# Seven block products in place of eight for half of the down projections' columns

## The chip, the cores and the metric

One core of a Trainium2 chip runs the whole program. The metric is the device time of one execution in microseconds (us); smaller is better. Weights come from HBM in every execution, as float32.

## What is computed

The reference is a two-layer decoder trunk over one sequence of 256 tokens with a model width of 2048. Each layer adds a mixer (layer 0: sliding-window attention beside a Mamba-2 scan; layer 1: dilated attention) and then an MLP. The change is in the MLPs alone:

```python
def squared_relu_mlp(h, w_up, w_down):
    u = jnp.einsum('bsd,df->bsf', h, w_up)
    return jnp.einsum('bsf,fd->bsd', jnp.square(jax.nn.relu(u)), w_down)

# every layer: x += mixer(rmsnorm(x)); x += squared_relu_mlp(rmsnorm(x))
# h: 256 x 2048, w_up: 2048 x 8192, w_down: 8192 x 2048
```

## The kernel before

**Products in three terms.** Every float32 operand is split in two parts of a shorter format (float32r): a high part, which is a rounded copy, and a low part, the rest. A product is the sum of high·high, high·low and low·high, so each product of a 128x128 block with a 128x512 block is three matmuls of 512 columns.

**Pieces.** `run` (line 229) works through one list, `todo`, of pieces. A piece is two k tiles of a weight (2 x 128 rows) by 512 columns, 512 KB. For each piece the SP queue loads it into `wraw` (`fetch`, line 233; 4 buffers, `RAW`), ScalarE (ACT in the profile) makes the high part `whi` (`high`, line 245; 5 buffers), and VectorE (DVE) subtracts it to make the low part `wlo` (`low`, line 252; 4 buffers). TensorE (PE) then does 12 matmuls: two k tiles, two halves of 128 tokens, three terms. At its place in the list, piece i first issues `low(i+2)`, `fetch(i+6)` and `high(i+3)`, then what is pending from the unit that ended (its `after`), and then its own matmuls.

**Units.** A unit is one 512-column stripe of one projection, all its k tiles in turn, with two PSUM banks `acc` (one for each 128 tokens).

**Side work.** Everything else (norms, attention, the MLP's activation) is a generator in `tasks`. `tick` (line 173), called once for each k tile, advances the tasks that are due, as long as a model of DVE's and ACT's load stays under a limit. `need` (line 187) does not wait for a due time: it advances the tasks in the order of the list, whatever their due times, until a label is in `done`. A unit calls it before the piece that reads what the label stands for. The order in which instructions are issued is the order on every engine's queue, since the scheduling is manual.

**The MLP** (`mlp`, line 847). There are 16 up units (`up(i)`, 8 pieces each) and 8 groups of four down units (`down(i)`, four stripes of 4 pieces, over the 8 k tiles that the up units 2i and 2i+1 give). The order is up 0, up 1, then for i from 1 to 7: up 2i, up 2i+1, down i-1; and down 7 at the end. So a period is 16 up pieces and 16 down pieces. When an up unit ends, `squared` (line 849) runs at its side: ACT applies ReLU from PSUM into `relu`, DVE squares it, PE transposes it in eight 128x128 steps into `uT` (PSUM), and `split` makes the high and low parts `uh` and `ul`. When a down unit ends, `add_stripe` (line 516) adds its two banks to `res`, the residual.

**Buffers.** `slot` tiles (`hThi`, `hTlo`, `uh`, `ul` and the like) share 18 buffers of 4 KB a partition, and `w4` tiles (`relu` and the like) share 11. PSUM has four `acc` banks and four `aux` banks.

Of the kernel before, what the change touches and what calls it, by code (L numbers as in the profile page):

```python
# [7 lines left out]
F32 = mybir.dt.float32  # L8
# [22 lines left out]
RAW = 4  # L31
AHEAD = 3
FREE = 1100.0
LIMIT = 1200.0
CAP = (2, 2, 2, 3)
XZ = ((0, 0), (1, 0), (0, 1), (2, 0), (1, 1), (3, 0), (2, 1), (3, 1))
# [3 lines left out]
def trunk(ctx: ExitStack, tc: tile.TileContext, x, norm_mix, norm_ffn, w_up, w_down, ab_w_in, ab_q_norm,  # L40
# [2 lines left out]
    nc = tc.nc  # L43
    consts = ctx.enter_context(tc.tile_pool(name="consts", bufs=1))
    wpool = ctx.enter_context(tc.tile_pool(name="weights", bufs=4))
    slots = ctx.enter_context(tc.tile_pool(name="slots", bufs=18))
    work = ctx.enter_context(tc.tile_pool(name="work", bufs=11))
    small = ctx.enter_context(tc.tile_pool(name="small", bufs=4))
    accs = ctx.enter_context(tc.tile_pool(name="accs", bufs=4, space=bass.MemoryType.PSUM))
    auxs = ctx.enter_context(tc.tile_pool(name="auxs", bufs=4, space=bass.MemoryType.PSUM))  # L50
# [24 lines left out]
    V, S, PE = Engine(nc.vector, "V", 90, 1.04), Engine(nc.scalar, "S", 240, 0.83), Engine(nc.tensor, "PE", 0, 0.84)  # L75

    def slot(name):
        return slots.tile([128, 4, T], F32R, name=name, tag="slot")

    def w4(shape, name):  # L80
        return work.tile(shape, F32, name=name, tag="w4")
# [88 lines left out]

    load = {"V": 0.0, "S": 0.0}

    def tick():
        clock[0] += 1
        for e in load:
            load[e] = max(0.0, load[e] - FREE)
        ran = []
        while max(load.values()) < LIMIT and len(ran) < 4:
            before = dict(spent)
            t = step(skip=ran)  # L180
            if t is None:
                break
            ran.append(t)
            for e in load:
                load[e] += spent[e] - before[e] - 0.5 * (spent["PE"] - before["PE"])

    def need(label):
        while label not in done:
            assert step(True) or label in done, label
# [30 lines left out]
            V.scalar_tensor_tensor(lo, src, gain, f32(hi), op0=OP.mult, op1=OP.subtract)  # L220


    units = []

    def unit(segs, ktiles, after, flip=False, needs={}):

        units.append((segs, ktiles, after, flip, needs))

    def run():
        todo = [(u, c) for u in units for c in range(0, len(u[1]), KC)]  # L230
        raws, parts = {}, {}

        def fetch(i):
            if i >= len(todo):
                return
            (segs, ktiles, *_), c = todo[i]
            kt = ktiles[c][0]
            raws[i] = raw = wpool.tile([128, KC, sum(s[2] for s in segs)], F32, name="wraw", bufs=RAW)
            o = 0
            for w, c0, m in segs:  # L240
                nc.sync.dma_start(raw[:, :, o:o + m],
                                  w[kt * 128:(kt + KC) * 128, c0:c0 + m].rearrange("(k p) c -> p k c", p=128))
                o += m

        def high(i):
            if i < len(todo):
                raw = raws[i]
                hi = wpool.tile([128, KC, raw.shape[2]], F32R, name="whi", bufs=AHEAD + 2)
                S.activation(hi, raw, AF.Copy)
                parts[i] = [hi]  # L250

        def low(i):
            if i < len(todo):
                raw = raws.pop(i)
                lo = wpool.tile([128, KC, raw.shape[2]], F32R, name="wlo", bufs=AHEAD + 1)
                V.tensor_tensor(lo, raw, f32(parts[i][0]), op=OP.subtract)
                parts[i].append(lo)

        for i in range(RAW):
            if i % 2 == 0:  # L260
                load_x(i // 2)
            fetch(i)
        for i in range(AHEAD):
            high(i)
            low(i)
            if i == 0:
                need(todo[0][0][4][0])
            if i % 2 == 0:
                load_x(2 + i // 2)
            fetch(RAW + i)  # L270
        high(AHEAD)
        nc.sync.dma_start(cst[:, C_TRI:], shapes[:, C_TRI:])
        pending = None
        before = ps = None
        kept, held = [], []
        for i, (u, c) in enumerate(todo):
            segs, ktiles, after, flip, needs = u
            n = sum(s[2] for s in segs)
            if i:
                low(i + AHEAD - 1)  # L280
                fetch(i + AHEAD - 1 + RAW)
                high(i + AHEAD)
            if pending is not None:
                pending[0](pending[1])
                pending = None
            if c == 0:
                if before is not None:
                    need(before)
                before = ps and id(ps)
                ps = [accs.tile([128, W], F32, name="acc") for _ in range(2)]  # L290
                kept.append(ps)
            if c in needs:
                need(needs[c])
            hi, lo = parts.pop(i)
            end = i == len(todo) - 1
            for k in range(KC):
                tick()
                first, last = c + k == 0, c + k == len(ktiles) - 1
                xh, xl, j = ktiles[c + k][1]()
                xh, xl = xh[:, j], xl[:, j]  # L300
                if flip:
                    for b in range(n // 128):
                        o = ps[b // 2][:, (b % 2) * T:(b % 2 + 1) * T]
                        wh, wl = hi[:, k, b * 128:(b + 1) * 128], lo[:, k, b * 128:(b + 1) * 128]
                        PE.matmul(o, wh, xh, start=first and b % 2 == 0, stop=False, skip_group_check=True)
                        PE.matmul(o, wh, xl, start=False, stop=False, skip_group_check=True)
# [12 lines left out]
            if c + KC >= len(ktiles):  # L319
                pending = after, ps  # L320
        pending[0](pending[1])


    class Norm:
# [196 lines left out]
                last(t, j)  # L521
        free(ps)

    def residual_units(w, ktiles, needs={}, nm=None, last=None):
        for j in range(NS):
            def after(ps, j=j):
                add_stripe(ps, j, last)
                if nm is not None:
                    nm.begin(j)

            unit([(w, j * W, W)], ktiles, after, needs=needs if j == 0 else {})


    win, wout = ab_w_in[0], ab_w_out[0]
# [306 lines left out]


    NB = FF // W

    def mlp(layer, nm, nxt, last=None):
        wu, wd = w_up[layer], w_down[layer]
        u = {}

        def squared(i, ps):
            yield from until(("rs", nm.row))  # L850
            r = w4([128, 2, W], "relu")
            for t in range(2):
                S.activation(r[:, t], ps[t], AF.Relu, scale=nm.rs_at(t))
            free(ps)
            yield 2
            V.tensor_tensor(r, r, r, op=OP.mult)
            yield 3
            u[i] = slot("uh"), slot("ul")
            for a in range(2):
                p = aux("uT")  # L860
                for b in range(2):
                    for t in range(2):
                        PE.transpose(p[:, b * T + t * 128:b * T + (t + 1) * 128],
                                     r[:, t, (2 * a + b) * 128:(2 * a + b + 1) * 128], ident)
                yield 1
                p = p.rearrange("p (b t) -> p b t", b=2)
                split(u[i][0][:, 2 * a:2 * a + 2], u[i][1][:, 2 * a:2 * a + 2], p)
                yield 2

        def after_up(i, ps):  # L870
            side(squared(i, ps), ("u", layer, i))

        def up(i):
            unit([(wu, i * W, W)], nm.ktiles(), lambda ps: after_up(i, ps), needs=nm.needs() if i == 0 else {})

        def down(i):
            kts = [(4 * (2 * i + b) + k, (lambda b=b, k=k: u[2 * i + b] + (k,))) for b in range(2) for k in range(4)]
            fin = i == NB // 2 - 1
            residual_units(wd, kts, {4 * b: ("u", layer, 2 * i + b) for b in range(2)}, nxt if fin else None,
                           last if fin else None)  # L880

        up(0)
        up(1)
        for i in range(1, NB // 2):
            up(2 * i)
            up(2 * i + 1)
            down(i - 1)
        down(NB // 2 - 1)

    n2 = Norm(R_MIX + 16, False)  # L890
    mlp(0, n1, n2)
# [111 lines left out]
```

## Time and profile before

| | |
|---|---|
| median of 3 runs | 2324.46 us (2324.34 to 2324.63) |
| profiled execution | 2324.46 us, of which its span (first to last instruction) is 2322.7 us |
| PE busy | 2310.5 us, 99% of the span |
| DVE busy | 1425.4 us, 61% |
| ACT busy | 1100.2 us, 47% |
| HBM read | 420.64 MB, 182 GB/s over the span |

Busy time of an engine is the time in which it had an instruction under way. PE's matmuls are pipelined: one is listed with some 0.39 us, while the next starts 0.23 us after it, so the mean duration of a matmul is not its cost; the distance between two starts is. PEld is the loading of PE's stationary operand, which runs beside the matmuls. PEclk (or PEclk in a view of stretches) is the clock that PE was granted, as a share of 2.4 GHz. A wait "A <- B" is the idle time of engine A that ended when B finished something.

### The profile page before, as it was taken

Reading aid. Unit: us, or ns where it says so; the run is one execution under the profiler, and the core shown is the slowest. Engines: PE = TensorE matmul, PEld = TensorE weight load, DVE = VectorE, ACT = ScalarE, POOL = GpSimd, SP = SyncE. Lnnn points to the kernel's source line nnn. Section 1 sums busy time; section 2 is a strip of 40 time slices with the busy share of each in tenths; the row PEclk is TensorE's granted clock in tenths of the full one; section 3 lists DMA queues with packets and bytes.
Section 4 is the critical chain, followed back from the end, with each engine's and each line's share of the span. In section 5 each row is a group of like instructions: output and inputs, shape, how many; then the busy total and the mean of one; then the engine's idle time right before and its main releaser. Section 6 shows DMA issues by size and latency. Waiting matters only on the chain.

```text
span 2322.7 us, 30056 instructions
## 1 busy us (share of the span) xinstructions
PE 2310.5 (99%) x11317; PEld 1928.3 (83%) x11317; DVE 1425.4 (61%) x2150; ACT 1100.2 (47%) x1411; POOL 8.4 (0%) x20
## 2 busy tenths in 40 slices
PE   8999999999999999999999999999999999999999
PEld 7999988888888888888888778778888888888887
DVE  6779986555555555555566766655555555555554
ACT  5565555444444444444454555554444444444442
POOL 1000000000000000000000000000000000000000
PEclk9999999999999999999999999999999999999999
DMA  7546655566666666666656555546656666656664
GB/s 231 163 145 191 180 174 181 190 188 184 191 187 190 192 183 191 192 188 191 190 179 184 155 154 171 165 160 183 189 185 189 191 189 191 190 184 194 191 185 162
DMA packets 229201, 424.73 MB, mean 183 GB/s; under 512 B 15620, under 2 KB 26160, under 8 KB 229056
## 3 DMA queue, kind: packets, MB, share of 16 engines
q1 hardware_dynamic: 218976, 416.34, 58.8%
q10 hardware_dynamic: 9568, 6.34, 0.9%
q8 instruction: 88, 1.44, 0.3%
q14 instruction: 57, 0.47, 0.1%
q0 software_dynamic: 512, 0.15, 0.0%
HBM read 420.64 MB, written 2.13 MB: 182 GB/s over the span
## 4 chain that ended last, share of the span: by engine, by line
PE 99%; DMA 0%; DVE 0%; ACT 0%; SPq 0%; issue 0%; ACTq 0%
PE acc L71 93%; PE uT L71 1%; PE sc L71 1%; PE o L71 1%; PE pT L71 1%; PE yp L71 1%; PE xT L71 1%; DMA wraw<-in_ab_w_in_dram 0%; PE qp L71 0%; PE yo L71 0%; PE kp L71 0%; PE xtok L71 0%; PE yT L71 0%; PE hst L71 0%; DVE wlo L71 0%; ACT whi L71 0%
## 5 line engine op out<-in xcount | busy, mean ns | idle before, releaser
L71 DVE TENSOR_TENSOR wlo<-wraw,whi 128x1024 fp32r<-128x1024 f32 (+1 forms) x792 | 962.3, 1218 | 611.3 <-PE acc L71 524.1
L71 ACT ACTIVATE whi<-wraw 128x1024 fp32r<-128x1024 f32 (+1 forms) x792 | 836.7, 1058 | 950.6 <-PE acc L71 831.9
L71 PE MATMUL acc<-whi,hThi 128*128 128x512 f32 (+1 forms) x1632 | 645.9, 396 | 2.6 <-ACT hThi L71 2.6
L71 PE MATMUL acc<-whi,hTlo 128*128 128x512 f32 (+1 forms) x1632 | 634.7, 389 | 0.3 <-DVE hTlo L71 0.3
L71 PE MATMUL acc<-wlo,hThi 128*128 128x512 f32 (+1 forms) x1632 | 634.0, 388 | 0.0
L71 PE MATMUL acc<-whi,uh 128*128 128x512 f32 x1024 | 401.5, 392 | 0.0
L71 PE MATMUL acc<-whi,ul 128*128 128x512 f32 x1024 | 398.8, 389 | 0.0
L71 PE MATMUL acc<-wlo,uh 128*128 128x512 f32 x1024 | 398.6, 389 | 0.0
L71 PEld LDWEIGHTS acc<-whi,hThi 128*128 128x128 f32 x1632 | 307.6, 188 | 68.0 <-issue 5.8
L71 PEld LDWEIGHTS acc<-whi,hTlo 128*128 128x128 f32 x1632 | 307.4, 188 | 64.8 <-DVE hTlo L71 0.9
L71 PEld LDWEIGHTS acc<-wlo,hThi 128*128 128x128 f32 x1632 | 307.9, 189 | 60.2 <-issue 1.0
L71 PEld LDWEIGHTS acc<-whi,ul 128*128 128x128 f32 x1024 | 192.2, 188 | 40.2
L71 PEld LDWEIGHTS acc<-wlo,uh 128*128 128x128 f32 x1024 | 192.4, 188 | 39.0
L71 PEld LDWEIGHTS acc<-whi,uh 128*128 128x128 f32 x1024 | 192.3, 188 | 38.8
L71 DVE TENSOR_TENSOR res<-acc,res 128x512 f32<-128x512 f32 x144 | 98.8, 692 | 78.1 <-PE acc L71 78.1
L71 PE MATMUL acc<-hThi,whi 128*128 128x256 f32 x384 | 112.3, 293 | 0.0
L71 PE MATMUL acc<-hThi,wlo 128*128 128x256 f32 x384 | 108.5, 283 | 0.0
L71 PE MATMUL acc<-hTlo,whi 128*128 128x256 f32 x384 | 108.5, 283 | 0.0
L71 DVE TENSOR_TENSOR ul<-uT,uh 128x512 fp32r<-128x512 f32 x64 | 44.3, 692 | 98.4 <-ACT uh L71 98.4
L71 ACT ACTIVATE uh<-uT 128x512 fp32r<-128x512 f32 x64 | 38.3, 598 | 90.5 <-PE uT L71 90.5
L71 PEld LDWEIGHTS acc<-hThi,whi 128*128 128x128 f32 x384 | 73.5, 191 | 3.4 <-issue 3.3
L71 PE MATMUL acc<-whi,mixh 128*128 128x512 f32 x192 | 75.6, 394 | 0.0
(200 smaller groups left out, 1577.0 us busy)
## 6 DMA issues: line engine op xcount, KB each, us to landing
wraw<-in_w_up_dram SPq DMA_DIRECT2D x256, 512.0 KB, 4.3
wraw<-in_w_down_dram SPq DMA_DIRECT2D x256, 512.0 KB, 4.3
wraw<-in_ab_w_in_dram SPq DMA_DIRECT2D x96, 512.0 KB, 3.7
wraw<-in_c_w_qkv_dram SPq DMA_DIRECT2D x96, 512.0 KB, 4.2
wraw<-in_ab_w_out_dram SPq DMA_DIRECT2D x48, 512.0 KB, 3.6
wraw<-in_c_w_o_dram SPq DMA_DIRECT2D x32, 512.0 KB, 3.6
wt<-cumd ACTq DMA_DIRECT2D x8, 512.0 KB, 6.8
res<-in_x_dram SPq DMA_DIRECT2D x4, 512.0 KB, 5.1
```

The source lines that it names most:

```text
L71: return f(out, *a, **k)
```

## The change

For seven of the eight groups of down units in each layer, the stripes 0 and 1 (columns 0 to 1023) are no longer two units. The product of a 2x2 block matrix (tokens: two halves of 128; k: the up units 2c and 2c+1) with a 2x2 block matrix (k: the same; columns: two stripes) is made from seven block products (class `Seven`) rather than eight.

- Each of the seven products takes two pieces with 6 matmuls each (two k tiles, three terms, one half of tokens) and gathers them in one `aux` bank `sp`; so 14 pieces with 84 matmuls stand for 8 pieces with 96.
- Weight blocks are loaded once, into `sraw` tiles (8 loads of 512 KB, as many as before). Four of the seven products take sums of weight blocks, which DVE forms in place (`add`, issued four pieces ahead): 8 additions of 128x1024.
- Two sums `s1` and `s2` of activations are formed by DVE (four subtractions of 128x512) and split in high and low parts.
- Each product is added to a block of `res`, or in the first group copied by ACT to a tile of its own (`evict`); the blocks of `res` are held in a transformed shape meanwhile, and `together` undoes that with seven additions of DVE after the last seven-product group.
- `squared` no longer squares on DVE: ACT squares while it reads `uT`, into `uf`. A second generator, `operands(c)`, makes `uh` and `ul` of both up units and the sums. It is started when the second up unit of the pair has ended, and it waits until the seven products and the two plain stripes of group c-1 have been issued.
- The order of a period is new: `rest` (up 2c+2, down stripes 2 and 3, up 2c+3; 24 pieces) with the 14 pieces of the seven products strewn in, none of them beside another one, from after the fifth piece to before the last. The eighth group is four plain units, as before, and follows up 15 at once.
- The two pools of 18 and 11 buffers become one of 29, in which the `sraw` tiles live too.

```diff
+HEAVY = 1200.0
...
-    slots = ctx.enter_context(tc.tile_pool(name="slots", bufs=18))
-    work = ctx.enter_context(tc.tile_pool(name="work", bufs=11))
+    work = ctx.enter_context(tc.tile_pool(name="work", bufs=29))
...
-    def tick():
+    def tick(heavy=False):
...
+        if heavy:
+            load["V"] += HEAVY
...
+    SEVEN = (("P1", "11", None), ("P2", "21", None), ("Q3", "22", None), ("Q5", "11", "12"), ("Q7", "12", "22"),
+             ("Q6", "11", "22"), ("Q4", "11", "21"))
...
+        def fetch(self, p, h):
+            _, block, other = SEVEN[p]
+            b = block if other is None else "12" if p == 3 else None
+            if b is not None:
+                r, c = self.rows[int(b[0]) - 1] + h * KC, self.c0 + (int(b[1]) - 1) * W
+                self.raw[b, h] = t = work.tile([128, KC, W], F32, name="sraw", tag="w4")
+                nc.sync.dma_start(t, self.w[r * 128:(r + KC) * 128, c:c + W].rearrange("(k p) c -> p k c", p=128))
+
+        def add(self, p, h):
+            _, block, other = SEVEN[p]
+            if other is not None:
+                t = self.raw[block, h]
+                V.tensor_tensor(t, t, self.raw[other, h], op=OP.add)
...
                 high(i + AHEAD)
-            if pending is not None:
-                pending[0](pending[1])
-                pending = None
+                add(i + AHEAD + 1)
+            for f in pending:
+                f()
+            pending = []
+            hi, lo = parts.pop(i)
+            if isinstance(u, Seven):
+                p, h = c
+                name = SEVEN[p][0]
+                if p in u.needs and h == 0:
+                    need(u.needs[p])
+                if h == 0:
+                    sp = aux("sp")
+                xh, xl, t0 = u.operands(name)
+                tick(True)
+                for k in range(KC):
+                    q = h * KC + k
+                    wh, wl = xh[:, q, t0:t0 + 128], xl[:, q, t0:t0 + 128]
+                    PE.matmul(sp, wh, hi[:, k], start=q == 0, stop=False)
+                    PE.matmul(sp, wh, lo[:, k], start=False, stop=False)
+                    PE.matmul(sp, wl, hi[:, k], start=False, stop=q == u.halves * KC - 1)
+                if h == u.halves - 1:
+                    pending.append(lambda u=u, name=name, sp=sp: u.evict(name, sp))
+                    if p == 6:
+                        done.add(u.mark)
+                continue
...
-            V.tensor_tensor(r, r, r, op=OP.mult)
-            yield 3
-            u[i] = slot("uh"), slot("ul")
+            uf[i] = w4([128, 4, T], "uf")
...
-                p = p.rearrange("p (b t) -> p b t", b=2)
-                split(u[i][0][:, 2 * a:2 * a + 2], u[i][1][:, 2 * a:2 * a + 2], p)
+                S.activation(uf[i][:, 2 * a:2 * a + 2], p.rearrange("p (b t) -> p b t", b=2), AF.Square)
+                yield 1
+
+        def operands(c):
+
+            if c:
+                yield from until(("seven", layer, c - 1))
+                yield from until(("rest", layer, c - 1))
+            for i in (2 * c, 2 * c + 1):
+                yield from until(("uf", layer, i))
+                u[i] = slot("uh"), slot("ul")
+                split(u[i][0], u[i][1], uf[i])
+                done.add(("u", layer, i))
                 yield 2
+            if c == NC - 1:
+                return
...
         def after_up(i, ps):
-            side(squared(i, ps), ("u", layer, i))
+            side(squared(i, ps), ("uf", layer, i))
+            if i % 2:
+                side(operands(i // 2), ("sums", layer, i // 2))
...
+        plan.extend(up(0) + up(1))
+        for c in range(NC - 1):
+            rest = up(2 * c + 2) + down(c, 2) + down(c, 3) + up(2 * c + 3)
+            s = seven(c)
+            for k, x in enumerate(rest):
+                while s and k >= 4.5 + (len(rest) - 4.5) / 14 * (14 - len(s)):
+                    plan.append(s.pop(0))
+                plan.append(x)
+            plan.extend(s)
+        for j in range(NS):
+            plan.extend(down(NC - 1, j))
```

## Rows read from the trace of the kernel before

**Rows 1.** The page, part 1: busy us (share of the span) xinstructions of each engine.

```profile
PE 2310.5 (99%) x11317; PEld 1928.3 (83%) x11317; DVE 1425.4 (61%) x2150; ACT 1100.2 (47%) x1411; POOL 8.4 (0%) x20
```

**Rows 2.** The waits, engine <- releaser: us in total, times, longest us.

```profile
ACT whi L71 <- PE acc L71: 831.9, 544, 5.3
DVE wlo L71 <- PE acc L71: 524.1, 355, 3.0
...
PE acc L71 <- ACT hThi L71: 2.6, 2, 2.1
```

**Rows 3.** One period of layer 1's MLP: busy us (instructions), clock, DMA share, GB/s.

```profile
1709.19:1798.13 88.94, 88.94 (x402) 73.68 (x401) 49.10 (x47) 38.72 (x40) 0.00 (x0) 1.00 0.62 190
```

**Rows 4.** The chain that ended last, in that period: start us, us, what.

```profile
1708.76 0.44 PE uT L71 x4
1709.19 61.24 PE acc L71 x270
```

**Rows 5.** Groups of instructions by shape: busy us, mean ns of one, idle before.

```profile
L71 DVE TENSOR_TENSOR wlo<-wraw,whi 128x1024 fp32r<-128x1024 f32 x784 | 956.2, 1223 | 604.8 <-PE acc L71 524.1 <-issue 68.8 <-ACT whi L71 3.4
L71 ACT ACTIVATE whi<-wraw 128x1024 fp32r<-128x1024 f32 x784 | 831.2, 1062 | 942.0 <-PE acc L71 831.9 <-DVE res L71 36.9 <-issue 34.1
...
L71 DVE TENSOR_TENSOR res<-acc,res 128x512 f32<-128x512 f32 x144 | 98.8, 692 | 78.1 <-PE acc L71 78.1
...
L71 ACT ACTIVATE relu<-acc,rs 128x512 f32<-128x512 f32 x64 | 43.9, 690 | 30.2 <-PE acc L71 30.2
L71 DVE TENSOR_TENSOR relu<-relu 128x1024 f32<-128x1024 f32 x32 | 39.0, 1220 | 0.0
L71 ACT ACTIVATE uh<-uT 128x512 fp32r<-128x512 f32 x64 | 38.3, 598 | 90.5 <-PE uT L71 90.5
```

**Rows 6.** The same view of stretches as in rows 3, in layer 0's input projection.

```profile
50.00:60.00 10.00, 10.00 (x47) 8.26 (x47) 9.31 (x29) 5.62 (x7) 0.00 (x0) 1.00 0.55 157
60.00:70.00 10.00, 10.00 (x47) 8.29 (x47) 9.59 (x24) 2.93 (x4) 0.00 (x0) 1.00 0.41 111
```

**Rows 7.** DMA: an issue group with KB and us to landing, and a stretch's GB/s.

```profile
wraw<-in_w_down_dram SPq DMA_DIRECT2D x256, 512.0 KB, 4.3
...
15.00:20.00 5.00, 2.76 (x15) 2.51 (x16) 3.21 (x7) 3.50 (x10) 0.00 (x0) 0.88 1.06 368
```

**Rows 8.** Order of time, PE and ACT, after an up unit: start us, us, what.

```profile
910.33 0.39 PE L71 MATMUL acc<-whi,hTlo 128*128 128x512 f32 x1
...
910.75 1.37 ACT L71 ACTIVATE relu<-acc,rs 128x512 f32<-128x512 f32 x2 [0.98 <-PE acc L71]
...
911.24 0.39 PE L71 MATMUL acc<-whi,hThi 128*128 128x512 f32 x1
...
918.04 0.60 PE L71 MATMUL uT<-cst,relu 128*128 128x128 f32 x4
...
918.67 0.60 ACT L71 ACTIVATE uh<-uT 128x512 fp32r<-128x512 f32 x1 [0.73 <-PE uT L71]
```

**Rows 9.** Order of time, PE's two longest waits after the start.

```profile
16.89 0.40 PE L71 MATMUL acc<-whi,hThi 128*128 128x288 f32 x1 [2.13 <-ACT hThi L71]
...
17.77 0.40 PE L71 MATMUL acc<-whi,hTlo 128*128 128x288 f32 x1 [0.35 <-DVE hTlo L71]
```

**Rows 10.** Stretches after those waits, as in rows 3; the clock is third from last.

```profile
18.50:19.00 0.50, 0.50 (x5) 0.50 (x4) 0.50 (x2) 0.00 (x0) 0.00 (x0) 0.79 1.15 365
19.00:20.00 1.00, 1.00 (x7) 0.98 (x6) 0.97 (x2) 0.00 (x0) 0.00 (x0) 0.50 1.10 354
20.00:21.00 1.00, 1.00 (x6) 1.00 (x5) 0.34 (x1) 0.57 (x1) 0.00 (x0) 0.50 0.97 238
21.00:22.00 1.00, 1.00 (x6) 1.00 (x5) 0.12 (x1) 1.00 (x4) 0.00 (x0) 0.50 0.76 223
22.00:22.50 0.50, 0.50 (x5) 0.50 (x4) 0.50 (x2) 0.50 (x3) 0.00 (x0) 0.80 0.94 365
```

**Rows 11.** The waits of the DMA queue SP, as in rows 2.

```profile
SPq L241 <- DVE wlo L71: 1857.4, 754, 7.8
```

More of the change, by code (lines that the diff above doesn't have):

```diff
@@ L77, in slot @@
     def slot(name):
-        return slots.tile([128, 4, T], F32R, name=name, tag="slot")
+        return work.tile([128, 4, T], F32R, name=name, tag="w4")
     def w4(shape, name):
@@ L220, in split, with __init__, unit, source @@
             V.scalar_tensor_tensor(lo, src, gain, f32(hi), op0=OP.mult, op1=OP.subtract)
-    units = []
-    def unit(segs, ktiles, after, flip=False, needs={}):
-        units.append((segs, ktiles, after, flip, needs))
+    plan = []
+    class Unit:
+        def __init__(self, segs, ktiles, after, flip=False, needs={}, mark=None):
+            self.segs, self.ktiles, self.after, self.flip, self.needs, self.mark = segs, ktiles, after, flip, needs, mark
+            self.n = sum(s[2] for s in segs)
+            self.pieces = [(self, c) for c in range(0, len(ktiles), KC)]
+    def unit(*a, **k):
+        plan.extend(Unit(*a, **k).pieces)
+    SEVEN = (("P1", "11", None), ("P2", "21", None), ("Q3", "22", None), ("Q5", "11", "12"), ("Q7", "12", "22"),
+             ("Q6", "11", "22"), ("Q4", "11", "21"))
+    class Seven:
+        def __init__(self, w, rows, c0, kts, operands, evict, needs, mark):
+            self.w, self.rows, self.c0, self.operands, self.evict, self.needs, self.mark = \
+                w, rows, c0, operands, evict, needs, mark
+            self.halves = kts // KC
+            self.raw = {}
+            self.pieces = [(self, (p, h)) for p in range(7) for h in range(self.halves)]
+        def fetch(self, p, h):
[10 more added lines that the diff above has]
+                V.tensor_tensor(t, t, self.raw[other, h], op=OP.add)
+        def source(self, p, h):
+            return self.raw[SEVEN[p][1], h]
     def run():
-        todo = [(u, c) for u in units for c in range(0, len(u[1]), KC)]
+        todo = plan
         raws, parts = {}, {}
@@ L235, in fetch @@
                 return
-            (segs, ktiles, *_), c = todo[i]
-            kt = ktiles[c][0]
-            raws[i] = raw = wpool.tile([128, KC, sum(s[2] for s in segs)], F32, name="wraw", bufs=RAW)
+            u, c = todo[i]
+            if isinstance(u, Seven):
+                u.fetch(*c)
+                return
+            kt = u.ktiles[c][0]
+            raws[i] = raw = wpool.tile([128, KC, u.n], F32, name="wraw", bufs=RAW)
             o = 0
-            for w, c0, m in segs:
+            for w, c0, m in u.segs:
                 nc.sync.dma_start(raw[:, :, o:o + m],
@@ L243, in fetch, with add @@
                 o += m
+        def add(i):
+            if i < len(todo) and isinstance(todo[i][0], Seven):
+                todo[i][0].add(*todo[i][1])
         def high(i):
             if i < len(todo):
+                u, c = todo[i]
+                if isinstance(u, Seven):
+                    raws[i] = u.source(*c)
                 raw = raws[i]
@@ L266, in run @@
             if i == 0:
-                need(todo[0][0][4][0])
+                need(todo[0][0].needs[0])
             if i % 2 == 0:
@@ L272, in run @@
         nc.sync.dma_start(cst[:, C_TRI:], shapes[:, C_TRI:])
-        pending = None
-        before = ps = None
+        pending = []
+        before = ps = sp = None
         kept, held = [], []
         for i, (u, c) in enumerate(todo):
-            segs, ktiles, after, flip, needs = u
-            n = sum(s[2] for s in segs)
             if i:
@@ L282, in run @@
                 high(i + AHEAD)
-            if pending is not None:
-                pending[0](pending[1])
-                pending = None
+                add(i + AHEAD + 1)
+            for f in pending:
+                f()
+            pending = []
+            hi, lo = parts.pop(i)
+            if isinstance(u, Seven):
+                p, h = c
[17 more added lines that the diff above has]
+                continue
+            segs, ktiles, flip, n = u.segs, u.ktiles, u.flip, u.n
             if c == 0:
@@ L291, in run @@
                 kept.append(ps)
-            if c in needs:
-                need(needs[c])
-            hi, lo = parts.pop(i)
+            if c in u.needs:
+                need(u.needs[c])
             end = i == len(todo) - 1
@@ L319, in run @@
             if c + KC >= len(ktiles):
-                pending = after, ps
-        pending[0](pending[1])
+                pending.append(lambda u=u, ps=ps: u.after(ps))
+                if u.mark is not None:
+                    done.add(u.mark)
+        for f in pending:
+            f()
     class Norm:
@@ L522, in add_stripe, with residual_unit, after, residual_units @@
         free(ps)
-    def residual_units(w, ktiles, needs={}, nm=None, last=None):
-        for j in range(NS):
[L526 to L531, printed above, removed]
+    def residual_unit(w, ktiles, j, needs={}, nm=None, last=None, pre=None, mark=None):
+        def after(ps):
+            if pre is not None:
+                need(pre)
+            add_stripe(ps, j, last)
+            if nm is not None:
+                nm.begin(j)
+        return Unit([(w, j * W, W)], ktiles, after, needs=needs, mark=mark)
+    def residual_units(w, ktiles, needs={}, nm=None):
+        for j in range(NS):
+            plan.extend(residual_unit(w, ktiles, j, needs if j == 0 else {}, nm).pieces)
     win, wout = ab_w_in[0], ab_w_out[0]
@@ L843, in trunk @@
     NB = FF // W
+    NC = NB // 2
     def mlp(layer, nm, nxt, last=None):
         wu, wd = w_up[layer], w_down[layer]
-        u = {}
+        uf, u, sums = {}, {}, {}
         def squared(i, ps):
@@ L865, in squared @@
                 yield 1
-                p = p.rearrange("p (b t) -> p b t", b=2)
-                split(u[i][0][:, 2 * a:2 * a + 2], u[i][1][:, 2 * a:2 * a + 2], p)
-                yield 2
+                S.activation(uf[i][:, 2 * a:2 * a + 2], p.rearrange("p (b t) -> p b t", b=2), AF.Square)
[9 more added lines that the diff above has]
+                done.add(("u", layer, i))
+                yield 2
+            if c == NC - 1:
+                return
+            a1, a2 = uf[2 * c], uf[2 * c + 1]
+            s1, s2 = w4([128, 4, T], "s1"), w4([128, 4, T], "s2")
+            o, n = slice(0, 128), slice(128, T)
+            V.tensor_tensor(s1[:, :, o], a1[:, :, n], a2[:, :, n], op=OP.subtract)
+            V.tensor_tensor(s1[:, :, n], a1[:, :, o], s1[:, :, o], op=OP.subtract)
+            V.tensor_tensor(s2[:, :, o], a1[:, :, n], a1[:, :, o], op=OP.subtract)
+            V.tensor_tensor(s2[:, :, n], a2[:, :, o], s1[:, :, n], op=OP.subtract)
+            yield 2
+            sums[c] = [(slot("sh"), slot("sl")) for _ in range(2)]
+            for (h, l), s in zip(sums[c], (s1, s2)):
+                split(h, l, s)
+                yield 1
@@ L870, in after_up @@
         def after_up(i, ps):
-            side(squared(i, ps), ("u", layer, i))
+            side(squared(i, ps), ("uf", layer, i))
+            if i % 2:
+                side(operands(i // 2), ("sums", layer, i // 2))
         def up(i):
[L874 to L888, printed above, removed]
+            return Unit([(wu, i * W, W)], nm.ktiles(), lambda ps: after_up(i, ps),
+                        needs=nm.needs() if i == 0 else {}).pieces
+        def down(c, j):
+            kts = [(4 * (2 * c + b) + k, (lambda b=b, k=k: u[2 * c + b] + (k,))) for b in range(2) for k in range(4)]
+            end = c == NC - 1
+            return residual_unit(wd, kts, j, {4 * b: ("u", layer, 2 * c + b) for b in range(2)},
+                                 nxt if end else None, last if end else None,
+                                 ("seven's sums", layer) if end and j < 2 else None,
+                                 ("rest", layer, c) if j == NS - 1 else None).pieces
@@ new lines, in mlp, with evict @@
+        keep = {}
+        R = [[res[:, t, j * W:(j + 1) * W] for j in range(2)] for t in range(2)]
+        def evict(c, name, ps):
+            if c == 0 and name == "P1":
+                keep["pq"], keep["q6"] = w4([128, 2, W], "pq"), w4([128, W], "q6")
+                keep["P1"], keep["Q5"], keep["Q6"] = keep["pq"][:, 0], keep["pq"][:, 1], keep["q6"]
+                V.tensor_tensor(R[1][0], R[1][0], R[1][1], op=OP.add)
+            if name in keep and c == 0:
+                S.activation(keep[name], ps, AF.Copy)
+            else:
+                r = {"P2": R[0][0], "Q3": R[0][1], "Q4": R[1][0], "Q7": R[1][1]}.get(name)
+                r = keep[name] if r is None else r
+                V.tensor_tensor(r, ps, r, op=OP.add)
+            if c == NC - 2 and name == "Q4":
+                side(together(), ("seven's sums", layer))
@@ new lines, in together @@
+        def together():
+            P1, Q5, Q6 = keep["P1"], keep["Q5"], keep["Q6"]
+            V.tensor_tensor(R[0][0], P1, R[0][0], op=OP.add)
+            V.tensor_tensor(P1, Q6, P1, op=OP.subtract)
+            V.tensor_tensor(R[1][1], P1, R[1][1], op=OP.add)
+            V.tensor_tensor(R[1][0], R[1][0], R[1][1], op=OP.subtract)
+            yield 2
+            V.tensor_tensor(P1, P1, Q5, op=OP.add)
+            V.tensor_tensor(R[0][1], P1, R[0][1], op=OP.add)
+            V.tensor_tensor(R[1][1], Q5, R[1][1], op=OP.add)
+            yield 1
@@ new lines, in seven, with parts @@
+        def seven(c):
+            def parts(name):
+                i, k, t = {"P1": (0, 0, 0), "P2": (0, 1, 0), "Q4": (0, 1, 128), "Q5": (1, 0, 0), "Q6": (1, 0, 128),
+                           "Q7": (1, 1, 0), "Q3": (1, 1, 128)}[name]
+                return (sums[c][k] if i else u[2 * c + k]) + (t,)
+            return Seven(wd, (8 * c, 8 * c + 4), 0, 4, parts, lambda name, ps: evict(c, name, ps),
+                         {0: ("u", layer, 2 * c), 1: ("u", layer, 2 * c + 1), 2: ("sums", layer, c)},
+                         ("seven", layer, c)).pieces
```

## The prediction, made before the changed kernel ran

> **What bounds the kernel now.** I read the busy times first: PE has an instruction under way for 2310.5 of 2322.7 us, DVE for 61% and ACT for 47% [rows 1]. A busy PE is not yet a bound, since its matmuls overlap, so the waits come next: DVE and ACT sit idle for 524.1 and 831.9 us until PE has used up an older weight part, while the other way round the longest entry of PE is 2.6 us [rows 2]. The two split engines are ahead of PE, and PE waits for nobody after the start (2322.7 - 2310.5 = 12.2 us of idle, in the first 18 us). Then one period of the MLP, between the ends of two equal up units: 88.94 us, PE busy in all of it at full clock, DVE 49.10 us (55%), ACT 38.72 us (44%) [rows 3]. Last the chain, for the price of a matmul: 270 in a row take 61.24 us, so 61.24 / 270 = 0.2268 us each, and four transposes 0.44 us, so 0.11 us each [rows 4]. Check: 384 x 0.2268 + 16 x 0.11 = 88.9 us, the period. So the time is the number of matmuls times 0.2268 us, and the questions are how many go and whether PE must wait for the first time.
>
> **What is removed.** Per group 96 matmuls of 512 columns become 84. They are of the same form as the others (128x128 stationary, 512 moving, a fresh stationary each time), so the price is that of rows 4. Seven groups in two layers: 14 x 12 = 168 matmuls, 168 x 0.2268 = 38.1 us. A period becomes 372 x 0.2268 + 1.76 = 86.1 us.
>
> The Trainium skill, page "TensorE: Matmul & The Clock Gate", section "Back-to-back issue gap", puts a lone stream of 512-column matmuls at 215.7 ns; by it the saving would be an estimated 36.2 us. The row of this trace is 226.8 ns, and it decides.
>
> **What is added on DVE.** Durations from [rows 5]. Low parts: 38 pieces instead of 32, 38 x 1.223 = 46.5 us. Sums of weight blocks: 8 of 128x1024; the nearest row is the squaring of `relu`, also float32 from SBUF to SBUF, 1.220, so 9.8. Evictions: seven products and four plain banks, 11 x 0.692 = 7.6 (`res` row). Low parts of `uh` from SBUF at 128x1024: 2 x 1.22 = 2.4. Subtractions for `s1`, `s2`: 4 x 0.692 = 2.8 (same row; no row has SBUF alone at this size, and half of the 1.220 row, 0.61, is the other bound). Their low parts: 2.4. Sum 71.5 us, and the squaring of `relu` is gone from it. That is 71.5 / 86.1 = 83% of the period, against 55%.
>
> ACT: 38 x 1.062 + 4 x 0.690 (ReLU) + 4 x 0.598 (square from PSUM, priced as the copy from PSUM `uh`; at most the ReLU's 0.690) + 4 x 1.06 (high parts of `u` and the sums) = 49.8 us, 58%, against 44%. Both stay under PE's time on the mean.
>
> **The tightest stretch.** The seven-product pieces are short for PE (6 x 0.2268 = 1.36 us against 2.72) and dear for DVE. The adds are issued from the fifth of them on. From there, each block on DVE's queue is a low part (1.22), plus an add (1.22) or an eviction (0.69, or 1.38 for two plain banks) where the order has one; in the order of issue: 2.4, 1.2, 2.6, 3.1, 1.2, 2.4, 1.2, 1.2, 3.1, 2.6, 2.4, 1.2, 2.4, 1.9, 1.2, 2.4 us. PE's pieces beside them are 1.36, 2.72, 1.36, 2.72, 1.36, 2.72, 2.72, 1.36, 2.72, 1.36, 2.72, 2.72, 1.36, 2.72, 1.36, 2.72: 32.9 us of DVE against 34.0 of PE, 97%. Adding work and subtracting PE's time, never below zero, the lag of DVE peaks at about 1.7 us. A low part must be there three pieces after its block may start; the shortest three are 1.36 + 2.72 + 1.36 = 5.4 us, less 1.22 for the operation itself leaves 4.2 us. So 1.7 us of lag is covered with 2.5 us to spare, and I take 0 for this term. The trace has a like case: DVE at 9.31 and 9.59 of 10 us and PE still busy for all of it [rows 6]. If the spare were gone, each period would pay what exceeds it; I keep 0 to 1.5 us for each of 14 periods in the range.
>
> **Loads.** The bytes are the same. The eight `sraw` loads fall into the first eight seven-product pieces: 18 pieces' loads, 9.4 MB, in 8 x 1.36 + 10 x 2.72 = 38 us, so 248 GB/s against 190 now [rows 3]. The start of the kernel moved 368 GB/s [rows 7], so the engines can. A load lands in 4.3 us [rows 7] and is issued six pieces ahead, about 13 us; block "12" is wanted by its add two pieces sooner than a plain load would be. Priced at 0.
>
> **The pool.** By count at most 27 to 28 of the 29 buffers are held at once, so no engine should wait for one. It can't gain either: in the mixers PE has no idle time to give back.
>
> **The end of each MLP, where PE waits.** In the groups before, five plain pieces lie between the end of an up pair and the first piece that reads it. The eighth group follows up 15 at once, but `operands(7)` is started only when up 15 has ended, so even `uh` of up 14 isn't there, and `need` pushes out in one go what is in the task list: the rest of `together`, all of `squared(15)`, then the split of up 14. PE finds the eight transposes ahead of the next matmul. From the moment E at which PE would begin the next piece, by [rows 8]: ReLU of the first bank starts 0.49 us before E (910.75 against 911.24) and two take 1.37, to E + 0.9; four transposes 0.60 to 1.5, the other four to 1.9; squares of 0.598 each to 2.1 and 2.7 (a square starts 0.03 us after its transposes, 918.04 + 0.60 to 918.67); the high part of up 14, 1.06, to 3.8; its low part 1.22, to 5.0, or 5.3 with DVE still at the additions of `together` (7 x 0.692 behind a 0.69 eviction and a low part). The first two matmuls need the high part, the third the low part. Undisturbed, the third would start at E + 8 x 0.11 + 2 x 0.2268 = E + 1.3. So the loss is 5.2 - 1.3 = 3.9 us a layer, 7.8 in all; bounds 2.9 (only the high part is late) and 4.5 (every hand-over a tenth slower).
>
> **The clock.** When PE waited 2.13 and 0.35 us at the start [rows 9], its granted clock was at 0.50 of full speed (1.2 GHz) from 18.6 to 22.1 us, by [rows 10] 0.2 + 3 + 0.2 = 3.4 us, and it worked half as fast: 1.7 us lost. Here PE idles for 3.7 of some 5.2 us. I count one such drop for each layer: 2 x 1.7 = 3.4 us; bounds 0 and twice that.
>
> The same page of the Trainium skill, section "HAM oscillation — how this bites in real kernels", says that idle gaps between bursts put the array back to half rate; the rows above agree.
>
> **Sum.** -38.1 + 7.8 + 3.4 = -26.9 us. The profiled execution is 2324.46 us, 1.76 of it outside the span and unchanged, and equals the median: 2324.46 - 26.9 = 2297.6 us, 0.988 of before.
>
> **The rivals.**
> - The clock stays at full speed through the two waits: 2324.46 - 38.1 + 7.8 = 2294.2. For it: some matmuls and transposes lie between; against it: the rows on the start. 0.15.
> - No wait at the two ends, so only the matmuls count: 2324.46 - 38.1 = 2286.4. It needs the operands to be issued earlier than I read them from the code; nothing in the trace speaks for it. 0.06.
> - DVE becomes late in the tight stretch: adds waiting for block "12" to land, or evictions holding up DVE's queue till PE has ended a product, take the 2.5 us of spare and 0.5 to 1.5 us more in each of 14 periods: 2297.6 + 7 to 21 = 2305 to 2319. For it: 83% on the mean and 97% there; against it: rows 6. 0.19.
> - The same with some 2 us a period eats the whole gain (26.9 / 14 = 1.9): within 0.2% of before. 0.04.
> - Slower: the one pool. An `sraw` load takes a buffer whose last reader has just been issued, SP stands at it, and every later load stands behind it, for SP's queue is in order and already spends 1857.4 us waiting for low parts [rows 11]. If that lets PE wait one landing time of 4.3 us in each period: 2297.6 + 14 x 4.3 = 2358. It decides from 2.3 us a period on (2329.1 is 0.2% over). Against it: six pieces of lead. 0.06.
> - The forecast itself: 0.50.
>
> That fewer matmuls are done than I count from the code, or as many as before, I hold to be excluded: 84 and 96 follow from the loops.
>
> **How the numbers follow.** About 0.2% (4.6 us) is what a measurement can tell from no change. Below 2319.8: forecast, first, second and third rival, 0.90; between 2319.8 and 2329.1: 0.04; above: 0.06. The range 2289 to 2316 leaves out the second rival, the last two and the top of the third, some 0.19; it holds the bounds of the end's wait (2 x 1.0 less, 2 x 0.6 more) and of the clock.
>
> **What would show it.** PE's matmuls of 512 columns are 168 fewer. Periods of 86.1 us with PE busy throughout and DVE at some 71 us. Two gaps of PE, each of some 4 us, behind up 15 of each layer, with ACT `relu`, `uf`, `uh` and DVE `ul` as releasers, and a clock under 1 soon after. Wrong would be: entries "PE <- DVE wlo" or "<- ACT whi" in the middle of the periods (third rival), or split engines waiting for DMA `sraw` (slower rival), or no gap at the ends.

## The result, and the profile after

| | before | after |
|---|---|---|
| median | 2324.40 us | 2297.66 us (2297.4 to 2298.8) |
| ratio | | 0.9886, 95% interval 0.9869 to 0.9903 |
| span of the profiled execution | 2322.7 us | 2295.9 us |
| PE instructions | 11317 | 11149, 168 fewer |
| one MLP period | 88.94 us | 86.22 us |
| DVE busy in it | 49.10 us | 68.01 us |

The forecast was 2297.6 us. The first line below is part 1 of the changed kernel's page, to be read beside [rows 1]. The second is one period of layer 1's MLP, from the ReLU of an up unit to that of the next equal one, to be read beside [rows 3]; the columns are the same.

```profile
PE 2277.0 (99%) x11149; PEld 1898.3 (83%) x11149; DVE 1692.5 (74%) x2418; ACT 1239.9 (54%) x1561; POOL 8.4 (0%) x20
...
1751.45:1837.67 86.22, 86.22 (x390) 71.41 (x389) 68.01 (x66) 48.18 (x52) 0.00 (x0) 1.00 0.62 196
```

PE is busy in every microsecond of the period, at full clock, with DVE at 79% of it and ACT at 56%. So nothing in the periods eats the saving. PE's own waits follow (us in total, times, longest); those below 1 us in total and those at the start of the kernel are left out.

```profile
PE acc L71 <- ACT uh L71: 3.4, 2, 1.7
...
PE acc L71 <- DVE ul L71: 1.7, 2, 0.9
```

There are two of each: one for each layer, on the high and on the low part of up 14. There is no entry on `wlo` or `whi` of a period. This is the place in layer 0, in order of time (start us, us, what, and in brackets the engine's idle time before it with its releaser), with the rows of PE, ACT and DVE as they bear on it. The tiles `pq` and `q` hold the three products that are not added to `res` at once.

```profile
1134.23 0.69 DVE L71 TENSOR_TENSOR res<-sp,res 128x512 f32<-128x512 f32 x1 [0.30 <-PE sp L71]
1134.84 0.68 DVE L71 TENSOR_TENSOR res<-pq,res 128x512 f32<-128x512 f32 x1
...
1136.27 1.37 ACT L71 ACTIVATE relu<-acc,rs 128x512 f32<-128x512 f32 x2 [0.98 <-PE acc L71]
...
1136.52 0.39 PE L71 MATMUL acc<-whi,hTlo 128*128 128x512 f32 x1
1137.01 0.33 PE L71 MATMUL uT<-cst,relu 128*128 128x128 f32 x1
1137.69 0.98 PE L71 MATMUL uT<-cst,relu 128*128 128x128 f32 x7 [0.35 <-ACT relu L71]
1138.27 1.08 ACT L71 ACTIVATE uf<-uT 128x512 f32<-128x512 f32 x2 [0.64 <-PE uT L71]
1139.24 2.01 ACT L71 ACTIVATE uh<-uf 128x1024 fp32r<-128x1024 f32 x2
1140.36 0.50 PE L71 MATMUL acc<-whi,uh 128*128 128x512 f32 x1 [1.68 <-ACT uh L71]
1140.68 2.35 DVE L71 TENSOR_TENSOR ul<-uf,uh 128x1024 fp32r<-128x1024 f32 x2
1141.95 0.80 PE L71 MATMUL acc<-whi,ul 128*128 128x512 f32 x1 [0.86 <-DVE ul L71]
```

The last matmul of up 15 starts at 1136.52, so E, the moment at which PE would begin the next piece, is 1136.75. The third matmul of the next piece starts at 1141.95, which is E + 5.20, as forecast. In layer 1 it is 2247.30, with E at 2242.09: 5.21. Undisturbed it would have been E + 1.33, so each wait costs 3.9 us. The clock comes next, in stretches as in [rows 10] (the clock is third from last):

```profile
1140.00:1141.00 1.00, 0.65 (x2) 0.30 (x2) 1.00 (x3) 1.00 (x2) 0.00 (x0) 1.00 0.64 164
1141.00:1142.00 1.00, 0.14 (x2) 0.05 (x1) 1.00 (x2) 1.00 (x2) 0.00 (x0) 0.82 0.87 338
1142.00:1143.00 1.00, 1.00 (x3) 0.81 (x4) 1.00 (x2) 0.20 (x1) 0.00 (x0) 0.50 0.02 8
1143.00:1144.00 1.00, 1.00 (x4) 0.81 (x3) 1.00 (x2) 0.00 (x0) 0.00 (x0) 0.50 0.09 16
1144.00:1145.00 1.00, 1.00 (x4) 0.81 (x3) 0.17 (x1) 0.00 (x0) 0.00 (x0) 0.50 0.00 0
1145.00:1146.00 1.00, 1.00 (x5) 0.77 (x5) 0.19 (x1) 0.01 (x1) 0.00 (x0) 0.97 0.39 63
```

PE fell to half its clock (1.2 GHz) for 0.4 + 3 + 0.06 = 3.4 us. The chain of layer 0 shows the price: 64 matmuls from 1141.95 on took 16.25 us in place of 64 x 0.2268 = 14.5, so 1.7 us; in layer 1, 70 took 17.78 in place of 15.9, so 1.9 us. The span's account: -38.1 (matmuls) + 7.8 (two waits) + 3.6 (clock) = -26.7 us; measured 2295.9 - 2322.7 = -26.8.

### The profile page after: what moved, and what is told of

It is laid out like the page before. It is cut to its first block, busy times and chain, and to the rows that moved or that the text cites. A ratio compares the mean times of both kernels' runs of the same rounds, so it can differ in the third digit from the quotient of the medians.

```text
span 2295.9 us, 29951 instructions
## 1 busy us (share of the span) xinstructions
PE 2277.0 (99%) x11149; PEld 1898.3 (83%) x11149; DVE 1692.5 (74%) x2418; ACT 1239.9 (54%) x1561; POOL 8.4 (0%) x20
## 4 chain that ended last, share of the span: by engine, by line
PE 98%; DVE 1%; DMA 0%; ACT 0%; issue 0%; SPq 0%; ACTq 0%
PE acc L71 81%; PE sp L71 12%; PE uT L71 1%; PE sc L71 1%; PE o L71 1%; PE pT L71 1%; PE yp L71 1%; PE xT L71 1%; DMA wraw<-in_ab_w_in_dram 0%; DVE res L71 0%; PE qp L71 0%; DVE wlo L71 0%; PE yo L71 0%; PE kp L71 0%; PE yT L71 0%; PE xtok L71 0%
## 5 line engine op out<-in xcount | busy, mean ns | idle before, releaser
L71 ACT ACTIVATE whi<-wraw 128x1024 fp32r<-128x1024 f32 (+1 forms) x680 | 717.4, 1056 | 641.4 <-PE acc L71 518.1
L71 DVE TENSOR_TENSOR wlo<-wraw,whi 128x1024 fp32r<-128x1024 f32 (+1 forms) x680 | 823.4, 1216 | 314.7 <-PE acc L71 227.5
L71 ACT ACTIVATE whi<-sraw 128x1024 fp32r<-128x1024 f32 x196 | 207.7, 1060 | 178.4 <-DVE sraw L71 151.1
L71 DVE TENSOR_TENSOR wlo<-sraw,whi 128x1024 fp32r<-128x1024 f32 x196 | 239.7, 1223 | 59.4 <-PE acc L71 30.4
L71 PE MATMUL acc<-whi,uh 128*128 128x512 f32 x576 | 228.7, 397 | 3.4 <-ACT uh L71 3.4
L71 PE MATMUL acc<-whi,ul 128*128 128x512 f32 x576 | 226.0, 392 | 1.7 <-DVE ul L71 1.7
L71 PE MATMUL acc<-wlo,uh 128*128 128x512 f32 x576 | 225.5, 391 | 0.0
L71 DVE TENSOR_TENSOR sraw<-sraw 128x1024 f32<-128x1024 f32 x112 | 136.6, 1220 | 0.0
L71 PE MATMUL sp<-whi,sh 128*128 128x512 f32 x224 | 87.1, 389 | 0.0
L71 PE MATMUL sp<-wlo,sh 128*128 128x512 f32 x224 | 87.1, 389 | 0.0
```

The lines of the kernel that those rows point to most:

```text
L71: return f(out, *a, **k)
```

## The experiments

Theory: the time is the number of matmuls times their price, plus what PE waits at the two MLP ends and what the clock adds behind these waits; DVE's added work lies under PE as long as the tight stretch has spare lag. Rivals: the waits belong to the seven products themselves; DVE's work costs time wherever it is; or DVE is under PE on the mean and only the mean counts.

**The change without its seven products.**

```diff
-            rest = up(2 * c + 2) + down(c, 2) + down(c, 3) + up(2 * c + 3)
-            s = seven(c)
+            rest = up(2 * c + 2) + down(c, 0) + down(c, 1) + down(c, 2) + down(c, 3) + up(2 * c + 3)
+            s = []
```

The sums of activations and the wait for group c-1's products go too.

> The rest of the change without its seven products: all stripes as plain units with eight block products, the square on ACT, operands() and the one pool kept. Theory: the matmuls that go and the wait at the two MLP ends are separate terms, so without the saving only the waits stay. The additions of together() are not in DVE's queue here, so the low part of up 14 comes some 0.2 us sooner: 2324.4 + 2 x (3.7 + 1.7) = 2335 us (2332 to 2337), with the two gaps of PE of some 4 us and 512-column matmuls as many as before. Rival: the gaps belong to the seven products (DVE still at their evictions and additions), then 2324 to 2326.

Measured 2333.86 us (2333.54 to 2334.15; ratio 1.004, 1.0025 to 1.0055). PE has 11317 instructions again, and it waits at the same two places for the same operands, with no evictions or additions of the products on DVE. So the waits do not need the seven products, which leaves the order and the late start of `operands` (the next run changes both), and they cost 9.4 us against the kernel before when they stand alone. The two kernels differ by 2333.86 - 2297.66 = 36.2 us, where the matmuls make 38.1. Most of the rest lies at the ends: the first wait on `ul` is 0.53 us in place of 0.86, and the clock did not drop alike:

```profile
1160.00:1161.00 1.00, 1.00 (x5) 0.80 (x5) 1.00 (x2) 0.34 (x1) 0.00 (x0) 1.00 0.00 0
1161.00:1162.00 1.00, 1.00 (x6) 0.82 (x5) 0.97 (x1) 0.00 (x0) 0.00 (x0) 1.00 0.00 0
...
2279.00:2281.00 2.00, 0.43 (x4) 0.20 (x2) 0.00 (x0) 1.97 (x4) 0.00 (x0) 0.91 0.04 15
2281.00:2282.00 1.00, 0.89 (x2) 0.50 (x2) 0.90 (x1) 1.00 (x3) 0.00 (x0) 0.50 0.00 0
...
2284.00:2285.00 1.00, 1.00 (x4) 0.81 (x3) 0.59 (x1) 0.00 (x0) 0.00 (x0) 0.50 0.00 0
...
2287.00:2288.00 1.00, 1.00 (x5) 0.82 (x4) 0.91 (x1) 0.95 (x1) 0.00 (x0) 0.76 0.67 258
```

Behind layer 0's wait the clock stayed full; behind layer 1's it was at half from about 2280.6 to 2287.5, 0.4 + 6 + 0.5 = 6.8 us, part of it with PE still waiting.

**Both up units first in the last seven-product group.**

```diff
             rest = up(2 * c + 2) + down(c, 2) + down(c, 3) + up(2 * c + 3)
+            if c == NC - 2:
+                rest = up(2 * c + 2) + up(2 * c + 3) + down(c, 2) + down(c, 3)
...
-            if c:
+            if 0 < c < NC - 1:
                 yield from until(("seven", layer, c - 1))
```

> In the last seven-product group of each layer both up units come ahead of the plain stripes 2 and 3, and operands(7) doesn't wait for group 6. Theory: the gap at the MLP's end and the drop of the clock behind it both go, and nothing takes their place: 2297.7 - 7.8 - 3.4 = 2286.4 us (2285 to 2289), no wait of PE on uh, ul or relu. Rival: the wait moves, because the splits of up 14 and 15 now fall into the stretch where DVE is 97% loaded by the prediction's count, and PE waits there for wlo: 2290 to 2298.

Measured 2286.35 us (2286.26 to 2286.57; ratio to before 0.9836, 0.982 to 0.9852). All of PE's waits in this kernel, but for one of 0.2 us in the attention, are at its start:

```profile
PE pp L71 <- DMA cst<-in_shapes_dram: 2.9, 1, 2.9
PE xT L71 <- DMA res<-in_x_dram: 2.6, 1, 2.6
PE acc L71 <- ACT hThi L71: 2.2, 3, 1.3
PE acc L71 <- DVE hTlo L71: 0.9, 3, 0.3
```

The wait went and did not come back elsewhere. This order gains 11.3 us on the changed kernel, and the two terms measured above, 7.8 and 3.6 us, come to 11.4. The whole saving of the matmuls, 38.1 us, is now in the time: 2324.4 - 2286.35 = 38.1. This version beats both kernels.

**More work for DVE, in the tight stretch and away from it.** The low part of some pieces is computed twice: in the first kernel of the eight pieces a period of the products with adds, in the second of eight pieces of up units. `twice` is, for up units from the third on, the first four pieces of even ones and the last four of odd ones.

```diff
                 V.tensor_tensor(lo, raw, f32(parts[i][0]), op=OP.subtract)
+                u, c = todo[i]
+                if isinstance(u, Seven) and c[0] >= 3:        # first kernel
+                if not isinstance(u, Seven) and c in u.twice:  # second kernel
+                    V.tensor_tensor(lo, raw, f32(parts[i][0]), op=OP.subtract)
```

> The low part of the weights of products four to seven (the ones with adds) is computed twice: 8 more operations of 128x1024 a period, some 9.3 us of DVE, in the tight stretch. Mean load of DVE rises from 67.9 to some 77 of 86.1 us, still under PE. Theory (a stretch counts, with some 2.5 us of spare lag): the lag of 1.7 us grows by 5 or more, PE waits for wlo some 2.5 us in each of 14 periods: 2297.7 + 35 = 2333 us (2315 to 2350). Rival (the mean counts): 2297.7 +- 2 us.

> The same 8 more operations a period, but on the pieces of the up units away from the tight stretch (first four pieces of the first up unit of a period, last four of the second). Same mean load of DVE as the run with them in the stretch. Theory (a stretch counts): the slack there takes them, 2297.7 +- 2 us. If any more work of DVE costs time, as much as the run with them in the stretch.

Measured 2312.89 us (2312.71 to 2314.06) in the stretch and 2300.98 us (2300.34 to 2301.79) elsewhere: 15.2 and 3.3 us over the changed kernel. Both lie outside of what the theory expected, the first below its 2315 and the second above its 2 us. One period of each, in the same view as above, the stretch first:

```profile
1844.77:1931.89 87.12, 86.74 (x390) 71.24 (x389) 77.08 (x74) 47.02 (x51) 0.00 (x0) 1.00 0.60 192
...
1752.09:1838.30 86.21, 86.21 (x390) 71.42 (x389) 77.00 (x74) 47.61 (x52) 0.00 (x0) 1.00 0.60 195
```

DVE does the same 77 us in both. In the second kernel they cost the period nothing. In the first they cost 0.9 us (87.12 against 86.22), and 14 periods of that are less than the 15.2 us. PE's idle time in that period, on `wlo`, is only 0.4 us; the rest shows as longer busy time (86.74 against 86.22, for the same 390 instructions). That is how a short wait would look, since a matmul is listed with 0.39 us where the next can start after 0.23. What is left of the 15.2 us, and the 3.3 us of the second kernel, lie at the two ends (PE rows of the first kernel, one for each layer; then of the second, with ACT's rows in layer 1):

```profile
1142.71 0.33 PE L71 MATMUL uT<-cst,relu 128*128 128x128 f32 x1 [2.11 <-ACT relu L71]
2257.70 0.33 PE L71 MATMUL uT<-cst,relu 128*128 128x128 f32 x1 [3.76 <-ACT relu L71]
...
1137.90 0.33 PE L71 MATMUL uT<-cst,relu 128*128 128x128 f32 x1 [1.16 <-ACT relu L71]
...
2244.12 1.06 ACT L71 ACTIVATE whi<-wraw 128x1024 fp32r<-128x1024 f32 x1 [4.12 <-DMA wraw<-in_w_down_dram]
2245.09 1.25 ACT L71 ACTIVATE relu<-acc,rs 128x512 f32<-128x512 f32 x2
...
2245.81 2.33 PE L71 MATMUL uT<-cst,relu 128*128 128x128 f32 x8 [2.87 <-ACT relu L71]
```

The third matmul of the last group starts at E + 6.8 and E + 9.1 us in the first kernel and at E + 5.8 and E + 8.3 in the second (layer 0, then layer 1), in place of E + 5.2. The clock was at half for 6.8 us in both layers of the first kernel, and for 3.4 and 10.2 us in the second.

The wait has a new first link: ReLU itself is late. It stands in ACT's queue behind a `whi` that waits for its weights to land. In layer 1 of the second kernel that load was issued at 2238.67, 0.1 us after a doubled low part had ended and set its buffer free. That is E - 4.1; in the changed kernel the same load was issued at 2235.22, E - 6.9. So DVE's lag comes back to PE by way of the load, ACT's queue and ReLU. In the second kernel the lag is also put right there: four of its eight operations stand in the last four up pieces of the period, which at the end of the MLP are those of up 15. The next two runs test whether it is the end that makes the difference.

> The order of last_group_ups_first, with the low parts of products four to seven computed twice (8 more DVE operations a period in the tight stretch). In dve_twice_in_stretch a period took 87.0 us in place of 86.2, so 14 x 0.8 = 11 us of its 15.2 lie in the periods, and the rest at the two ends, where DVE's lag makes ACT late. Theory: with the ends mended only the periods stay: 2286.4 + 11 = 2297.5 us (2295 to 2300). Rival: the whole 15.2 us come back wherever the end is: 2301.6.

> The same order, with the 8 more operations a period on up pieces instead. In dve_twice_elsewhere the periods stayed at 86.2 us, so its 3.3 us lie at the two ends alone. Theory: with the ends mended nothing is left, 2286.4 +- 1 us. Rival (DVE's work costs a little everywhere): 2289.7.

Measured 2296.27 us (2295.25 to 2296.9) and 2286.45 us (2286.01 to 2286.87), against 2286.35 for the same order without the extra work. With the ends mended, 9 us of DVE a period on the up pieces are free, and in the stretch they cost (2296.27 - 2286.35) / 14 = 0.7 us a period. So a mean load is no measure of what DVE's work costs, and neither is its place within the period alone: lag that a period would absorb is paid for where PE meets a chain with no cover.

**How much the stretch can take.** The same line once more, so three times.

> The same order, the low parts of products four to seven computed three times: 16 more operations a period, 8 of them beyond the run that did it twice. Theory: the spare of the stretch is used up by the first eight (0.8 us over), so each further one is paid in full, at 1.15 us from one start to the next: 14 x (0.8 + 8 x 1.15) = 140 us, 2426 us (2400 to 2440). Rival: DVE's mean load decides; 67.9 + 16 x 1.15 = 86.3 of 86.2 us, so only about what twice costs, 2286 to 2300.

Measured 2434.11 us (2433.56 to 2434.8), 10.6 us a period more than with the order alone. A period, and PE's waits in total:

```profile
1900.23:1997.40 97.17, 89.26 (x390) 70.78 (x389) 86.60 (x81) 46.70 (x51) 0.00 (x0) 1.00 0.53 174
...
PE sp L71 <- DVE wlo L71: 69.0, 68, 1.8
PE acc L71 <- DVE wlo L71: 31.7, 42, 1.2
```

The second eight cost (2434.11 - 2296.27) / 14 / 8 = 1.23 us each: all of an operation. The first eight cost 0.09 us each. DVE is idle for 10.6 us of this period, so its mean load is not what binds; the stretch is. This is the third rival of the prediction made real, and it shows from where on it is: the stretch takes in some 8 us more of DVE's time before PE pays.

**A shorter chain at the end.**

```diff
-            if i % 2:
+            if i == NB - 2 or i % 2 and i != NB - 1:
                 side(operands(i // 2), ("sums", layer, i // 2))
```

> The changed kernel with one edit: operands(7) is started when up 14 has ended, not up 15, so the split of up 14 is issued before the plain units begin, and PE has two pieces of matmuls (5.4 us) before it needs up 15. Theory: the wait moves behind those two pieces and is shorter: the transposes, square, high and low part of up 15 that are then pushed out take to 3.6 us after the piece's start against 0.9 undisturbed, 2.7 us lost in place of 3.9; 2297.7 - 2 x 1.2 = 2295.3 us if the clock still drops, 2292 if it doesn't. Rival: the wait is as long as before (2297.7), because DVE's queue and not the order of the splits sets it.

Measured 2294.1 us (2291.9 to 2294.58). The waits of PE are 1.83 us on `uh` and 0.53 us on `ul` in both layers, and yet the clock differs (layer 0, then layer 1):

```profile
1145.12 0.50 PE L71 MATMUL acc<-whi,uh 128*128 128x512 f32 x1 [1.83 <-ACT uh L71]
1148.00:1149.00 1.00, 1.00 (x4) 0.81 (x3) 0.00 (x0) 0.00 (x0) 0.00 (x0) 0.50 0.56 68
...
2249.59 0.50 PE L71 MATMUL acc<-whi,uh 128*128 128x512 f32 x1 [1.83 <-ACT uh L71]
2252.00:2253.00 1.00, 1.00 (x6) 0.83 (x5) 0.00 (x0) 0.00 (x0) 0.00 (x0) 1.00 0.34 127
```

So the time lies between the forecast with two drops (2295.3) and without (2292). The chain gives 40 matmuls in 10.99 us after the first wait, 1.9 us too many, and 106 in 24.31 after the second, 0.3 too many. The execution of 2291.9 us is the one with a mean clock of 1.000, against 0.999 in the other three.

## Why the prediction was right

- **The saving.** 168 matmuls at 0.2268 us, 38.1 us. Shown by the order with both up units first, which has it whole. By the gap that the Trainium skill, page "TensorE: Matmul & The Clock Gate", section "Back-to-back issue gap", gives for matmuls of 512 columns taken by themselves, it would be an estimated 36.2 us; that run disagrees with it. The distance in this kernel's own chain was the right price.
- **The end of the MLP.** Read from the code and priced by rows, 3.9 us for each layer: measured 3.9 in both. The order with both up units first takes it away, and the change without its products keeps it, so cause and size are shown.
- **The clock.** 3.4 us in all was forecast, 3.6 measured, but the agreement is partly luck, and with it that of the whole sum to 0.1 us: in two other kernels one of the two waits left the clock alone. The bounds of 0 and twice that were the sounder statement.
- **DVE.** That its work stays under PE's was right, but its size was not: 71.5 us a period forecast, 68.0 measured. The count of operations holds (65, and 66 in the period's row). The step that failed is the price of one: its listed duration is not its cost when DVE's instructions stand back to back. In the tight stretch of the period above, an operation listed with 1.22 us is followed by the next after 1.14 (1768.09 to 1769.23), and one listed with 0.68 after 0.60:

```profile
1768.09 1.22 DVE L71 TENSOR_TENSOR sraw<-sraw 128x1024 f32<-128x1024 f32 x1
1769.23 0.68 DVE L71 TENSOR_TENSOR res<-sp,res 128x512 f32<-128x512 f32 x1
1769.83 1.21 DVE L71 TENSOR_TENSOR wlo<-wraw,whi 128x1024 fp32r<-128x1024 f32 x1
```

By these prices (1.14 and 0.60) the prediction's own count of the stretch, over the same blocks, gives 30.4 us of DVE in place of 32.9, and 3.1 us to spare in place of 2.5. By the same rule over a whole period, eight more low parts then exceed the spare by 0.7 us, and sixteen by 9.2; by the listed durations it would be 4.0 and 13.4. The runs gave 0.7 to 0.9 and 10.6. (The counted figures are estimates from these rows.) So the rule of the lag was sound. The run with the work doubled in the stretch, where some 2.5 us a period were expected, was over-priced for the most part by the price of an operation. ACT was over-sized as well, 49.8 against 48.2.

- **Loads and the pool.** Priced at 0, and PE waits for neither. But the `sraw` loads take 5.9 us to land, where 4.3 was taken from [rows 7]. The slower rival, SP standing at a buffer of the pool, did not come: at the line that issues the `sraw` loads (259) SP waited 2.4 us in all, and its waits for low parts are 1813.0 us, less than the 1857.4 of [rows 11].

```profile
sraw<-in_w_down_dram SPq DMA_DIRECT2D x112, 512.0 KB, 5.9
...
SPq L285 <- DVE wlo L71: 1813.0, 629, 7.8
...
SPq L259 <- PE acc L71: 2.4, 2, 1.2
```

## What to carry to other kernels

Where one engine is busy all the time and waits for nobody, a change's gain is the work taken from that engine at its start-to-start price; then walk the new order for the places where its next instruction hangs on a chain that has just begun, for there the gain leaks. Price added work on another engine by the stretch in which it stands, not by the mean, and at its start-to-start price too; and look at where lag that the stretch leaves behind is met. If a wait is found at the seam of two stages, first try to put already covered work between the producer and its reader: here one swap of order in one group gave back 11.3 us of the 38.1.

## What the runs showed of the hardware

- The drop of PE's clock behind a wait of the same make is not the same each time (layer 0, then layer 1): 3.4 us at half clock in both layers of the changed kernel, none and 6.8 us without the seven products, 3.4 us and none with the shorter chain. With the shorter chain PE idled for 1.83 and 0.53 us in both layers, with the same work between, and in the profiled execution the clock fell in one. What decides is left open; a forecast should carry it as a range.
- DVE operations that stand back to back start closer together than their listed durations: 1.14 us for 128x1024, listed with 1.22, and 0.60 us for 128x512, listed with 0.69. Where an addition needs the result of the one before it, the distance was 0.73 us (1135.55 to 1136.28).
